# Half of one late store of an attention kernel, issued by GpSimd in seven pieces of 17 rows

## The chip, the cores and the metric

The kernel runs on one core of a Trainium2 chip. The time is that of one execution on the device, in microseconds (us); a median of several runs is given with its range.

## The reference

Cross-covariance attention over 8 batches and 12 heads, 512 positions, 64 channels. The attention matrix of a head is only 64 x 64: the columns of Q and K are normalised over the positions, multiplied, put through a softmax, and the rows of V are multiplied by the result.

```python
Q_norm = Q / (np.linalg.norm(Q, axis=-2, keepdims=True) + 1e-10)
K_norm = K / (np.linalg.norm(K, axis=-2, keepdims=True) + 1e-10)
attn = np.einsum('bhnd,bhne->bhde', Q_norm, K_norm)
attn = np.exp(attn - np.max(attn, axis=-1, keepdims=True))
attn = attn / (np.sum(attn, axis=-1, keepdims=True) + 1e-10)
return np.einsum('bhnd,bhde->bhne', V, attn)
```

All tensors are float32. Q, K and V together are 37.75 MB to read, the output is 12.58 MB to write.

## The kernel before

The 96 heads are taken in 24 units of four heads, two units to a step s (12 steps), two steps to a wide step w of V (6 of them). A step loads Q and K (`qk32`), casts them to bf16 on DVE (`cast_qk`), and multiplies them on PE into Gram matrices (`grams`), which hold both the norms and the products. DVE, ACT and GpSimd turn these into the softmax weights `ab` (`squares` to `normalise`; GpSimd does `scale_k`, the tile `kqs`). V is cast to bf16, mostly by GpSimd (`cast_v`), transposed on PE (`vtrans`) and copied back (`vcopy`). `outs` multiplies it by `ab` into PSUM, and `ocopy` copies the result to the tiles `so` in SBUF, two copies to a tile, on ACT or, late in the program, also on DVE.

A step has two such tiles, i = 0 and 1, and each leaves in one transfer by SP's queue (`store`): 128 partitions, and on each two rows r = 0 and 1 of 2,048 bytes (J = 8 positions of 64 channels), 512 KB in all. Only the last tile, (11, 1), leaves as two transfers of half that size. There are thirteen buffers for `so`, so from store (5, 1) on, the last thirteen, no buffer is used again.

The order in which every engine issues its work is made by a planner, the class `Order`: each piece has costs, predecessors and a due time, and the planner writes out one order for all engines. It reckons with at most eight transfers in flight (`QUEUE = 8`). In the built program, too, each transfer of SP's waits, before it is issued, for the transfer eight before it, whose completion count it takes over. All loads are issued by SP, but two at the start by ACT. GpSimd issues none. At the end of the program SP waits for all the transfers that are still out.

```python
def store(s, i, k=None):
    rows = slice(None) if k is None else slice(k * (J // 2), (k + 1) * (J // 2))
    o = Of[s // 2, s % 2, i].rearrange("p r (j d) -> p r j d", d=D)
    nc.sync.dma_start(out=o[:, :, rows], in_=so[s, i][:, :, rows])
```

Of the kernel before, what the change touches and what calls it, by code (L numbers as in the profile page):

```python
# [102 lines left out]
def kernel(  # L103
# [7 lines left out]
    nc = tc.nc  # L111
# [3 lines left out]
    S = U // 2  # L115
# [3 lines left out]
    ONE = 3  # L119
    HELD, UNTIL = ("lk", 1, 1), ("cq", 0, 1)  # L120
    BOTH = S - 8

# [36 lines left out]
    qk32, v32, vb, qkb, gram, scr, kq, n2, r8, kqs, rq, lg, ex, ab, vps, vt, po, so = ({} for _ in range(18))  # L161
# [35 lines left out]
    def store(s, i, k=None):  # L197
        rows = slice(None) if k is None else slice(k * (J // 2), (k + 1) * (J // 2))
        o = Of[s // 2, s % 2, i].rearrange("p r (j d) -> p r j d", d=D)
        nc.sync.dma_start(out=o[:, :, rows], in_=so[s, i][:, :, rows])  # L200

    def cast_qk(u, x):
# [138 lines left out]
    for i in range(NB["ab"]):  # L341
        a = const.tile([128, HU, 2 * D], BF16, name=f"ab{i}")
# [17 lines left out]
    def piece(key, engines, after, behind, rank, fn, *args):  # L360
        if key[0] in ("cv", "vc", "oc", "kq", "sc"):
            plan.add(key, engines, after, behind, rank, lambda eng: fn(eng, *args))
        else:
            plan.add(key, engines, after, behind, rank, lambda eng: fn(*args))

    def back(kind, i, n, *rest):
        return (kind, i - n, *rest) if i - n >= 0 else None
# [17 lines left out]
    for u in range(U):  # L385
        s, r = divmod(u, 2)
# [21 lines left out]
    for w in range(W):  # L408
        both = 2 * w >= BOTH
        for r in range(2):  # L410
# [24 lines left out]
    for s in range(S):  # L435
        for x in range(4):
            i, k = divmod(x, 2)
            n = 4 * s + x - 2
            wait = [("oc", n // 4, n % 4)] if n >= 0 else []
            order = [("ou", s, x - 1) if x else back("ou", s, 1, 3)]  # L440
            piece(("ou", s, x), {"PE": 0.5}, [("vc", s // 2, *t) for t in turns(s // 2) if t[0] // 2 == k] + [("nm", s)] + wait, order, R["ou"] + 0.01 * s, outs, s, x)
            n = 2 * s + i - NB["so"]
            free = [("st", n // 2, n % 2)] if k == 0 and n >= 0 else []
            order = [("oc", s, x - 1) if x else back("oc", s, 1, 3)]
            piece(("oc", s, x), {"ACT": 0.6, "DVE": (0.68, BIAS["oc"])} if s >= BOTH else {"ACT": 0.6}, [("ou", s, x)] + free, order, R["oc"] + 0.01 * s, ocopy, s, x)
        for i in range(2):
            order = [("st", s, 0) if i else back("st", s, 1, 1)]
            if (s, i) == (S - 1, 1):

                piece(("sh", s, i), {"DMA": 0.67}, [("oc", s, 2)], order, v_at(2 * s + i) + ST_LAG, store, s, i, 0)  # L450
                piece(("st", s, i), {"DMA": 0.67}, [("oc", s, 3)], [("sh", s, i)], v_at(2 * s + i) + ST_LAG, store, s, i, 1)
            else:
                piece(("st", s, i), {"DMA": X}, [("oc", s, 2 * i), ("oc", s, 2 * i + 1)], order, v_at(2 * s + i) + ST_LAG, store, s, i)
# [43 lines left out]
```

## Time and profile before

| | |
|---|---|
| median of 3 runs | 128.83 us (128.76 to 129.06) |
| profiled execution, its own time | 129.06 us |
| its span in the profile | 127.3 us |
| busy: PE, DVE, ACT, POOL (GpSimd) | 62%, 73%, 57%, 28% of the span |
| moved by the DMA engines | 50.64 MB, mean 398 GB/s |
| transfers `out_dram<-so` by SP | 23 of 512 KB, two of 256 KB |
| last copy into `so` ends | 115.4 us |
| last issue of a store by SP | 117.3 us |

The profile shows one execution. Its page has the busy time of each engine, the span in 40 slices of 3.18 us (digits are tenths of a slice, 9 is 90% or more), the DMA queues, and the groups of instructions that cost most. A table of windows gives the same for chosen stretches, in us from the start of the span, with the mean share of time in which the sixteen DMA engines were busy; 1.05 stands for all of them, as the records of consecutive packets overlap a little. The time line lists instructions in order of time. "SPq" is SP issuing transfers; the time up to their landing is not in it.

### The profile page before, as it was taken

To read this page: it belongs to the slowest core of one execution; us is meant where nothing else is said; L and a number is where in the kernel's file an instruction comes from. 1 tells how busy PE (TensorE), PEld (TensorE's weight loads), DVE (VectorE), ACT (ScalarE), POOL (GpSimd) and SP (SyncE) were. 2 spreads that over 40 slices of the span, in tenths; PEclk is the share of its full clock that TensorE was granted. 3 is DMA by queue.
4 is the path that set the end of the run, shared out by engine and by line. 5 is a ranking of instruction groups with operands and counts; after the bars stand their busy time and mean duration, and the time that the engine had idled before them with its cause. 6 is when DMAs were issued, how large, how long until landed. Compare 5 with 4: busy or idle time off the path is not lost.

```text
span 127.3 us, 4884 instructions
## 1 busy us (share of the span) xinstructions
PE 79.4 (62%) x2128; PEld 64.0 (50%) x2128; DVE 93.0 (73%) x141; ACT 72.5 (57%) x220; POOL 36.3 (28%) x40
## 2 busy tenths in 40 slices
PE   0065384894844589859873996698975869580000
PEld 0055372773633568648661885486764748460000
DVE  3263649959999899998986798999999799820000
ACT  4000441569777068785792789384949969972000
POOL 4005306300915913033064203213453361200000
PEclk9999999999997556995999589655699995955555
DMA  3999999999999999999999999999999999999992
GB/s 107 404 434 409 430 409 418 415 440 402 425 429 416 407 418 424 407 416 422 430 415 409 417 424 417 417 420 424 406 413 407 406 401 406 400 407 407 408 352 98
DMA packets 15605, 50.64 MB, mean 398 GB/s; under 512 B 1120, under 2 KB 1632, under 8 KB 14176
## 3 DMA queue, kind: packets, MB, share of 16 engines
q1 hardware_dynamic: 15296, 49.29, 96.2%
q10 hardware_dynamic: 288, 1.05, 2.1%
q8 instruction: 16, 0.26, 0.7%
q14 instruction: 5, 0.04, 0.1%
HBM read 37.75 MB, written 12.58 MB: 396 GB/s over the span
## 4 chain that ended last, share of the span: by engine, by line
DVE 31%; DMA 20%; PE 18%; ACT 14%; issue 4%; SPq 2%; POOL 1%; DVEq 0%; POOLq 0%; ACTq 0%
DMA qk<-in_K_dram 14%; PE gram L226 12%; DVE qkb L206 11%; DVE scr L233 6%; DMA qk<-in_Q_dram 5%; DVE ab L284 5%; ACT so L165 4%; ACT vt L165 4%; ACT ex L275 4%; PE vps L295 3%; DVE vt L167 3%; DVE n L245 3%; PE po L312 2%; ACT kq L165 1%; SPq L184 1%
## 5 line engine op out<-in xcount | busy, mean ns | idle before, releaser
L226 PE MATMUL gram<-qkb 32*128 32x128 bf16 (+1 forms) x1504 | 35.6, 255 | 21.9 <-DVE qkb L206 8.8
L206 DVE CAST qkb<-qk 128x1024 bf16<-128x1024 f32 x48 | 37.3, 801 | 8.5 <-DMA qk<-in_Q_dram 7.0
L226 PEld LDWEIGHTS <-qkb 32*128 32x128 bf16 (+1 forms) x1504 | 29.8, 114 | 26.8 <-DVE qkb L206 11.6
L169 POOL TENSOR_SCALAR vb<-v 128x1024 bf16<-128x1024 f32 x19 | 21.2, 1126 | 45.1 <-DMA v<-in_V_dram 45.0
L165 ACT COPY so<-po 128x512 f32<-128x512 f32 x45 | 25.0, 593 | 6.6 <-PE po L312 6.4
L165 ACT COPY vt<-vps 128x1024 bf16<-128x1024 bf16 (+1 forms) x18 | 17.8, 987 | 15.9 <-PE vps L295 15.9
L312 PE MATMUL po<-ab,vt 128*64 128x128 bf16 x384 | 21.1, 259 | 6.0 <-issue 2.4
L295 PE MATMUL vps<-identb,vb 128*128 128x128 bf16 x192 | 19.3, 255 | 5.1 <-POOL vb L169 3.1
L256 POOL TENSOR_TENSOR kqs<-kq,r 64x512 f32<-64x512 f32 x12 | 13.7, 1143 | 26.9 <-ACT r L252 13.7
L312 PEld LDWEIGHTS <-vt 128*64 128x64 bf16 x384 | 15.3, 131 | 10.3 <-issue 5.4
L233 DVE SCALAR_TENSOR_TENSOR scr<-gram,eye 64x512 f32<-64x512 f32 x24 | 16.5, 688 | 4.7 <-PE gram L226 4.4
L295 PEld LDWEIGHTS <-vb 128*128 128x128 bf16 x192 | 14.1, 113 | 9.0 <-POOL vb L169 4.5
L275 ACT ACTIVATE ex<-lg,rq 128x64 f32<-128x64 f32 x48 | 14.5, 321 | 2.8 <-PE lg L269 2.8
L165 ACT COPY kq<-gram 64x512 f32<-64x512 f32 x12 | 7.0, 580 | 13.6 <-DVE scr L233 13.4
L284 DVE TENSOR_TENSOR ab<-ex,rinv 64x256 bf16<-64x256 f32 x24 | 13.2, 548 | 0.6
L275 ACT ACTIVATION_READ_ACCUMULATOR ex<-lg,rq 128x1 f32 x48 | 10.2, 213 | 0.0
L167 DVE CAST vb<-v 128x1024 bf16<-128x1024 f32 x5 | 7.4, 1483 | 1.3 <-DMA v<-in_V_dram 1.2
L269 PE MATMUL lg<-eye,kqs 64*128 64x64 f32 x48 | 6.9, 274 | 2.3 <-POOL kqs L256 1.8
L245 DVE TENSOR_REDUCE n<-scr 128x8 f32<-128x512 f32 x12 | 8.2, 679 | 0.1
L167 DVE COPY vt<-vps 128x1024 bf16<-128x1024 bf16 (+1 forms) x8 | 7.9, 1019 | 0.1
L269 PEld LDWEIGHTS lg<-eye,kqs 64*128 64x128 f32 x48 | 4.8, 168 | 4.3 <-POOL kqs L256 2.5
L281 DVE RECIPROCAL rinv<-esum 128x4 f32<-128x4 f32 x12 | 2.1, 172 | 2.6 <-ACT ex L275 2.5
(17 smaller groups left out, 16.0 us busy)
## 6 DMA issues: line engine op xcount, KB each, us to landing
out_dram<-so SPq DMA_DIRECT2D x23, 512.0 KB, 10.2
v<-in_V_dram SPq DMA_DIRECT2D x11, 1024.0 KB, 17.2
qk<-in_Q_dram SPq DMA_DIRECT2D x8, 1024.0 KB, 17.5
qk<-in_K_dram SPq DMA_DIRECT2D x8, 1024.0 KB, 18.5
qk<-in_Q_dram SPq DMA_DIRECT2D x8, 512.0 KB, 12.2
qk<-in_K_dram SPq DMA_DIRECT2D x6, 512.0 KB, 12.4
qk<-in_K_dram ACTq DMA_DIRECT2D x2, 512.0 KB, 6.3
v<-in_V_dram SPq DMA_DIRECT2D x2, 512.0 KB, 10.6
```

The source lines that it names most:

```text
L165: nc.scalar.copy(o, i)
L167: nc.vector.tensor_copy(o, i)
L169: nc.gpsimd.tensor_scalar(out=o, in0=i, scalar1=1.0, scalar2=0.0, op0=ALU.mult, op1=ALU.add)
L206: nc.vector.tensor_copy(qkb[u][:, :, x * D:(x + 1) * D], qk32[s][:, x, r])
L226: nc.tensor.matmul(gram[s][:, h, r, 0], x, x, start=(t == 0), stop=(t == (T if u < WIDE else J) - 1))
L233: nc.vector.scalar_tensor_tensor(out=scr[s][half], in0=gram[s][half, :, :, 0, half].rearrange("p h r d -> p (h r) d"), scalar=1e-20, in1=e ...
L245: nc.vector.tensor_reduce(out=n2[s], in_=scr[s], axis=mybir.AxisListType.X, op=ALU.add)
L256: (nc.vector if eng == "DVE" else nc.gpsimd).tensor_tensor(out=kqs[s][HI], in0=kq[s][HI], in1=r8[s][HI, :, None].to_broadcast([D, 2 * HU, ...
L275: nc.scalar.activation(e[:, h, :], lg[s][:, h, :], AF.Exp, scale=rq[s][:, h:h + 1], accum_out=z[:, h:h + 1])
L284: nc.vector.tensor_tensor(out=a[half, :, half], in0=e[half], in1=ri[half, :, None].to_broadcast([D, HU, D]), op=ALU.mult,)
L295: nc.tensor.transpose(ps[:, c, n, :], vb[w][:, J * c + j].rearrange("p r d -> p (r d)"), identb)
L312: nc.tensor.matmul(po[s, x][e * D:(e + 1) * D, j].rearrange("p r d -> p (r d)"), v, ab[s][:, h, :])
```

## The change

The store of tile (9, 1), the sixth transfer from the end, is split. S is 12, so `FEW` is (9, 1). Of its row r = 0, the partitions 0 to 118 go out in seven transfers of 17 partitions, issued by GpSimd; the partitions 119 to 127 go in one transfer by SP. The row r = 1 goes with all 128 partitions in one transfer by SP. The planner still plans one store at this place, and all other stores are as they were.

```diff
     BOTH = S - 8
+    FEW = (S - 3, 1)
...
     def store(s, i, k=None):
         rows = slice(None) if k is None else slice(k * (J // 2), (k + 1) * (J // 2))
         o = Of[s // 2, s % 2, i].rearrange("p r (j d) -> p r j d", d=D)
+        if (s, i) == FEW:
+
+            for a in range(0, 119, 17):
+                nc.gpsimd.dma_start(out=o[a:a + 17, 0], in_=so[s, i][a:a + 17, 0])
+            nc.sync.dma_start(out=o[119:, 0], in_=so[s, i][119:, 0])
+            nc.sync.dma_start(out=o[:, 1], in_=so[s, i][:, 1])
+            return
         nc.sync.dma_start(out=o[:, :, rows], in_=so[s, i][:, :, rows])
```

## The prediction

> **What bounds the kernel now.** I read the page first: the slices, then the table of the DMA queues.
>
> ```profile
> PE   0065384894844589859873996698975869580000
> DVE  3263649959999899998986798999999799820000
> DMA  3999999999999999999999999999999999999992
> q1 hardware_dynamic: 15296, 49.29, 96.2%
> q8 instruction: 16, 0.26, 0.7%
> ```
>
> From the second slice to the last but one, the sixteen DMA engines are full, while every compute engine is idle for the last four slices (12.7 us). The bytes set the time. One engine moves 409/16 = 25.6 GB/s (next view), so a packet of 2,048 bytes costs it 0.08 us, and a store of 512 KB (sixteen such packets on each engine) 1.28 us. Row q8 is instruction fetching: 0.7% of 16 x 127.3 us is 14.3 us in 16 packets, 0.9 us each, on single engines. That is the one thing here that isn't spread evenly.
>
> Second, the end in windows (from:to, then the engines, then the clock, the DMA share and GB/s):
>
> ```profile
> 120.00:122.00 2.00, 0.00 (x0) 0.00 (x0) 0.00 (x0) 0.00 (x0) 0.00 (x0) 0.50 1.05 404
> 122.50:123.00 0.50, 0.00 (x0) 0.00 (x0) 0.00 (x0) 0.00 (x0) 0.00 (x0) 0.50 0.96 358
> 123.00:123.50 0.50, 0.00 (x0) 0.00 (x0) 0.00 (x0) 0.00 (x0) 0.00 (x0) 0.50 0.80 299
> 123.50:124.00 0.50, 0.00 (x0) 0.00 (x0) 0.00 (x0) 0.00 (x0) 0.00 (x0) 0.50 0.68 260
> 124.00:124.50 0.50, 0.00 (x0) 0.00 (x0) 0.00 (x0) 0.00 (x0) 0.00 (x0) 0.50 0.55 205
> 124.50:125.00 0.50, 0.00 (x0) 0.00 (x0) 0.00 (x0) 0.00 (x0) 0.00 (x0) 0.50 0.53 186
> 125.00:125.50 0.50, 0.00 (x0) 0.00 (x0) 0.00 (x0) 0.00 (x0) 0.00 (x0) 0.50 0.55 195
> 125.50:126.00 0.50, 0.00 (x0) 0.00 (x0) 0.00 (x0) 0.00 (x0) 0.00 (x0) 0.50 0.22 74
> ```
>
> A share of 1.05 is all sixteen. At 124 us it is 0.55, so 16 x 0.55/1.05 = 8.4: eight engines are done and eight still work at full rate, until about 125.8 us. The sixteen completion counts of the last store in the trace say the same: eight arrive between 123.10 and 124.60 us, eight between 125.87 and 126.29. Sixteen fetches of 0.9 us, if they fall twice on each of eight engines, give 1.8 of the 2.4 us between the two means (123.7 and 126.1). The kernel ends when the late eight do. The mean of all sixteen is 124.9 us: perfect balance could give 126.3 - 124.9 = 1.4 us and no more.
>
> Third, when the moved work can start, from the time line (start, length):
>
> ```profile
> 107.83 1.04 POOL L256 TENSOR_TENSOR kqs<-kq,r 64x512 f32<-64x512 f32 x1 [3.75 <-ACT r L252]
> 108.65 1.07 ACT L165 COPY so<-po 128x512 f32<-128x512 f32 x2
> ```
>
> The order of the program shows that nothing moves on PE, DVE or ACT. GpSimd gets seven transfers behind its last instruction, which ends at 108.9 us. They wait for the second of the two ACT copies, which fills store (9, 1) and ends at 109.7. So they start at 109.8, beside 12.5 us in which the engines are full anyway. (The line shows the two copies as a group of x2; 108.65 + 1.07 is the end of the second.)
>
> **The change part by part.** The bytes stay the same. Before, every engine had 16 rows of store (9, 1), eight of each half. After, the second half still goes eight to an engine. The first half, 128 rows, goes as 119 in seven transfers of 17, and 9.
>
> No transfer of before has fewer than 128 rows, so no row shows where these go. The bounds: a transfer of 17 rows is spread (one or two rows per engine, and the balance stays), or sits on one engine (17 x 0.08 = 1.36 us of work). The nearest row is the q8 packet, which does sit on one engine. I take the second, and seven different engines for the seven. The nine rows of SP add at most one row to an engine, as one row can't be split further than a packet.
>
> The Trainium skill (DMA: Bandwidth & Descriptors, "Why a DMA increments its semaphore by 16 and not by 1") says that the number of engines is the largest up to 16 that divides the row count: 1 for 17, 9 for 9, and that GpSimd's transfers take consecutive engines in turn while SP's take the lowest-numbered. It also names an exception in which GpSimd gives each engine the row count over 16, rounded up: two rows here, so nine engines. By the first rule seven engines gain 10 rows; by the second eight gain 7. No run here shows either.
>
> So each of seven engines has 17 rows instead of 8 (+9), or +10 with one of SP's nine: +0.72 to +0.80 us. Each of the other nine engines loses 8, or 7 with a row of SP's: -0.64 to -0.56 us.
>
> If the seven are all among the early eight, the early ones end at 124.60 + 0.80 = 125.40 at worst, the late ones at 126.29 - 0.64 to - 0.56, that is 125.65 to 125.73. The late ones still end last, and the gain is 0.6 us.
>
> Issuing on GpSimd: no transfer of GpSimd's is in the trace. Nearest rows: SP's issues of the same tile, 0.37 us at the shortest, and GpSimd's own instructions of 1.04 to 1.14 us. I take 1.0, the engine's own row: 7 x 1.0 from 109.8 ends at 116.8. That costs nothing: the early engines are busy until 122.7 with queued stores, and the extra rows only have to be there before that. Cover is lost at (122.7 - 109.8)/7 = 1.84 us each.
>
> SP: two transfers in place of one. SP issues each transfer only when the one eight before it has landed, which is why its issues in the last stretch stand 1.28 us apart (109.56, 110.84, 112.17). One more transfer takes one of these eight places, so everything behind, stores (10, 0) to (11, 1), is issued one landing later: the last at 118.6 instead of 117.3. An early engine reaches the last store at 122.4, 3.8 us later. In the first slice 107 GB/s x 3.18 us = 340 KB moved, 0.8 us at 420 GB/s, so packets flowed by 2.4 us after an issue at 0.7: 1.7 us. That fits under 3.8, and costs nothing; without it the last store would start late by the difference.
>
> The end: SP closes with one wait after another, 0.06 us apart in the trace. Seven new completion counts, waited for in pairs, add up to four waits, 0 to 0.24 us if they stand behind the last landing. I take 0.12.
>
> Sum: -0.60 + 0.12 = -0.48 us. The profiled execution took 129.06 us (span 127.3 and 1.8 around it), so 128.58; it lay 0.23 over the median of 128.83, so against that 128.35 us.
>
> A rule against the change stands in the same page of the Trainium skill ("Rules for kernel authors"): spreading transfers over issuing engines brings no bandwidth, since they share the sixteen DMA engines. The row of 1.05 agrees that there is no bandwidth to win, and by the rule alone the gain would be zero; but the rows behind 122.5 us show unequal ends, which the rule doesn't speak of.
>
> **The rivals.** First, the seven transfers hit late engines. No view carries an engine's number. For the forecast: early and late are eight and eight, as if one half of the engines did the fetching, and seven loaded engines fit inside the other half, if they are taken in order from its start. Against: if the fetching engines are spread between the others, or are the half that is taken first, at least one late engine is loaded. One suffices: 125.87 to 126.29 + 0.72 to 0.80, at most 0.80 over today's end. With 0.12 for the waits that is 128.83 + 0.92 = 129.75 us, slower. It decides from the first late engine in the set.
>
> Second, the 17 rows are spread over all engines, or so that one of the latest is not relieved: the balance hardly moves, 0 to +0.24 for the waits, 128.8 to 129.0.
>
> Third, GpSimd issues slowly (it hasn't issued one in this program before). Above 1.84 us each it ends the kernel: at 2.5 us the last is out at 109.8 + 17.5 = 127.3, its 1.36 us of rows end at 128.7 where 125.8 was the end, +2.9, 131.7 us. For it speaks nothing but the absence of a row.
>
> **How the numbers follow.** A measurement of this kernel can tell about 0.2% (0.26 us) from no change. Forecast 0.48: the time lies in 128.1 (-0.64, no wait, and the 0.07 by which the fastest run lies under the median) to 128.5. Rival one 0.34, rival two 0.12, rival three 0.06. Rival two gives 0.10 to "same" and 0.02 to "slower"; so faster 0.48, same 0.10, slower 0.42. The range for eight in ten has to reach rival one: 128.1 to 129.85; it leaves out rival three and the edges.
>
> **What would show it.** Right: the DMA share stays at 1.05 to about 123, later than now on the early side, and falls to zero by 125.2 to 125.3 instead of 125.8; a new queue with 119 packets of 2,048 bytes; GpSimd's issues done by 117; SP's last issue near 118.6. Wrong by rival one: a few engines alone busy to 126.6, a share of 0.1 to 0.4 behind 125.8. Wrong by rival two: the same windows as now. Wrong by rival three: GpSimd issuing behind 122 us, and a gap before the last packets.

## The result and the profile after

The changed kernel took 129.16 us (median of 11 runs, 128.97 to 129.28), the kernel before, on the same chip, 128.88 us (128.76 to 129.06): a ratio of 1.0017, interval 1.0009 to 1.0024. By the ratio it is 0.22 us slower (0.12 to 0.31 by its interval; the medians lie 0.28 us apart). The forecast had been 0.48 us faster. The time lies in the range, on the other side of no change.

The profiled execution took 129.17 us, with a span of 127.4. First the table of the DMA queues, with GpSimd's new queue q0, and the group of its issues:

```profile
q1 hardware_dynamic: 15186, 49.04, 95.6%
q8 instruction: 16, 0.26, 0.7%
q0 software_dynamic: 224, 0.24, 0.5%
L204 POOL DMA_DIRECT2D out_dram<-so x7 | 3.7, 541 | 1.1 <-ACT so L166 1.1
```

The 224 packets of q0 are 32 for each of the seven transfers. By size in the trace, each has eight packets of 4,096 bytes, one of 2,052, seven of 8 and sixteen of 4. So a transfer of 17 rows did not leave as 17 rows on one engine: the sizes fit eight engines that took two rows each and a ninth that took one. Issuing took 0.51 us a transfer (0.7 for the first), from 111.7 to 115.4 us, and the rows had landed by 120.0: this part is off the path, as forecast.

Then the end, in windows (from:to, the engines, the clock, the DMA share, GB/s):

```profile
122.50:123.00 0.50, 0.00 (x0) 0.00 (x0) 0.00 (x0) 0.00 (x0) 0.00 (x0) 0.50 1.01 379
123.50:124.00 0.50, 0.00 (x0) 0.00 (x0) 0.00 (x0) 0.00 (x0) 0.00 (x0) 0.50 0.75 277
124.00:124.50 0.50, 0.00 (x0) 0.00 (x0) 0.00 (x0) 0.00 (x0) 0.00 (x0) 0.50 0.70 252
124.50:125.00 0.50, 0.00 (x0) 0.00 (x0) 0.00 (x0) 0.00 (x0) 0.00 (x0) 0.50 0.61 217
125.00:125.50 0.50, 0.00 (x0) 0.00 (x0) 0.00 (x0) 0.00 (x0) 0.00 (x0) 0.50 0.35 121
125.50:126.00 0.50, 0.00 (x0) 0.00 (x0) 0.00 (x0) 0.00 (x0) 0.00 (x0) 0.50 0.15 53
126.00:126.50 0.50, 0.00 (x0) 0.00 (x0) 0.00 (x0) 0.00 (x0) 0.00 (x0) 0.50 0.01 4
```

Up to 125 us the share is higher than before (0.70 against 0.55 at 124): early engines work longer. From 125 to 126 it is lower (0.35 against 0.55, 0.15 against 0.22): most late engines stop sooner. But 0.15 is still 16 x 0.15/1.05 = 2.3 engines, and the last row now reaches past 126. The completion counts of the last store in the trace (one from each engine, when its share has landed) say it by engine: six at 125.38 to 125.67, one at 126.00, and two at 126.41 and 126.43. Before, the eight late ones stood at 125.87 to 126.29. So six late engines were relieved by about 0.6 us, as forecast, and a pair was not. The one at 126.00 got rows too: followed back as the third from the last of each store (125.35, 124.70, 123.43, 122.16, 120.90), it leads to 120.40, the third from the last of the nine counts of SP's transfer of nine rows. The experiments below will show only two late engines among these nine, so it is the slowest of the early ones.

### The profile page after: what moved, and what is told of

It reads as the page before. It is cut to its first block, busy times and chain, and to the rows that moved or that the text cites. A ratio compares the mean times of both kernels' runs of the same rounds, so it can differ in the third digit from the quotient of the medians.

```text
span 127.4 us, 4896 instructions
## 1 busy us (share of the span) xinstructions
PE 78.3 (61%) x2128; PEld 64.4 (51%) x2128; DVE 90.7 (71%) x141; ACT 72.3 (57%) x220; POOL 40.8 (32%) x47
## 3 DMA queue, kind: packets, MB, share of 16 engines
q10 hardware_dynamic: 288, 1.05, 2.2%
## 4 chain that ended last, share of the span: by engine, by line
DVE 37%; PE 31%; issue 12%; ACT 6%; DMA 5%; SPq 0%; DVEq 0%; ACTq 0%
PE gram L234 17%; DVE qkb L214 17%; DVE scr L241 8%; PE po L320 7%; DMA qk<-in_Q_dram 5%; PE vps L303 5%; DVE ab L292 5%; DVE vt L168 3%; DVE n L253 2%; ACT so L166 2%; ACT vt L166 2%; PE lg L277 1%; DVE so L168 1%; ACT ex L283 1%; ACT kq L166 1%
## 5 line engine op out<-in xcount | busy, mean ns | idle before, releaser
L234 PE MATMUL gram<-qkb 32*128 32x128 bf16 (+1 forms) x1504 | 37.0, 262 | 25.5 <-DVE qkb L214 10.5
L234 PEld LDWEIGHTS <-qkb 32*128 32x128 bf16 (+1 forms) x1504 | 31.4, 117 | 29.9 <-DVE qkb L214 12.9
L170 POOL TENSOR_SCALAR vb<-v 128x1024 bf16<-128x1024 f32 x19 | 22.4, 1193 | 32.2 <-DMA v<-in_V_dram 29.0
L303 PE MATMUL vps<-identb,vb 128*128 128x128 bf16 x192 | 18.0, 246 | 3.5 <-POOL vb L170 2.1
L303 PEld LDWEIGHTS <-vb 128*128 128x128 bf16 x192 | 13.5, 110 | 6.6 <-POOL vb L170 2.5
L292 DVE TENSOR_TENSOR ab<-ex,rinv 64x256 bf16<-64x256 f32 x24 | 14.6, 609 | 0.6
L277 PE MATMUL lg<-eye,kqs 64*128 64x64 f32 x48 | 6.4, 258 | 4.2 <-POOL kqs L264 2.2
L204 POOL DMA_DIRECT2D out_dram<-so x7 | 3.7, 541 | 1.1 <-ACT so L166 1.1
```

Of the source, the lines that this page charges most:

```text
L170: nc.gpsimd.tensor_scalar(out=o, in0=i, scalar1=1.0, scalar2=0.0, op0=ALU.mult, op1=ALU.add)
L234: nc.tensor.matmul(gram[s][:, h, r, 0], x, x, start=(t == 0), stop=(t == (T if u < WIDE else J) - 1))
L277: nc.tensor.transpose(l[:, h, :], kqs[s][HI, 2 * h:2 * h + 2].rearrange("p r d -> p (r d)"), eye2[HI])
L292: nc.vector.tensor_tensor(out=a[half, :, half], in0=e[half], in1=ri[half, :, None].to_broadcast([D, HU, D]), op=ALU.mult,)
L303: nc.tensor.transpose(ps[:, c, n, :], vb[w][:, J * c + j].rearrange("p r d -> p (r d)"), identb)
```

## The experiments

Theory A: the kernel ends later because some of the engines that got more rows are among those that end late anyway. Rival B: transfers issued by GpSimd cost time by themselves. Rival C: SP's additional transfer does. All kernels but the last are the changed one with other lines for the first half (r = 0) of store (9, 1); the second half stays with SP unless said otherwise. Every ratio is against runs of the kernel before on the same chip, whose medians were 128.90 to 128.94 us.

**Who issues, with the balance kept.** Two controls, `e_pool128` and `e_sp128`:

```diff
-            for a in range(0, 119, 17):
-                nc.gpsimd.dma_start(out=o[a:a + 17, 0], in_=so[s, i][a:a + 17, 0])
-            nc.sync.dma_start(out=o[119:, 0], in_=so[s, i][119:, 0])
+            nc.gpsimd.dma_start(out=o[0:128, 0], in_=so[s, i][0:128, 0])   # e_pool128
+            nc.sync.dma_start(out=o[0:128, 0], in_=so[s, i][0:128, 0])     # e_sp128
```

> The first half of store (9, 1) leaves by GpSimd in one transfer of 128 rows, eight rows to each DMA engine as before; SP sends the second half. Theory A (the changed kernel is slower because some of the engines that got more rows are among the eight that end late): the balance is that of before, so 128.9 us, within 0.1. Rival B (a transfer issued by GpSimd costs time by itself, whatever its shape): 129.1 us or more, as in the changed kernel.

> SP sends store (9, 1) as two halves of 128 rows; GpSimd sends nothing. Theory A and rival B: 128.9 us, within 0.1, as nothing is uneven and GpSimd is out of it. Rival C (the additional transfer of SP, which takes one of its eight places, costs the time): 129.1 us.

Measured: 129.03 us, ratio 1.0005 (0.9996 to 1.0014), and 128.91 us, ratio 0.9997 (0.9988 to 1.0006). Rival C is out. One transfer by GpSimd costs nothing that can be told.

**Rows on the lowest engines, by SP.** Here SP sends the first half in transfers whose row counts put 17 rows on each of the first seven, six or five engines: `e_sp119` with 119 and 9 rows, `e_sp102` with 102, 16 and 10, `e_sp85` with 85, 32 and 11. The edit for the last:

```diff
-            for a in range(0, 119, 17):
-                nc.gpsimd.dma_start(out=o[a:a + 17, 0], in_=so[s, i][a:a + 17, 0])
-            nc.sync.dma_start(out=o[119:, 0], in_=so[s, i][119:, 0])
+            nc.sync.dma_start(out=o[0:85, 0], in_=so[s, i][0:85, 0])
+            nc.sync.dma_start(out=o[85:117, 0], in_=so[s, i][85:117, 0])
+            nc.sync.dma_start(out=o[117:128, 0], in_=so[s, i][117:128, 0])
```

> The 119 rows leave by SP in one transfer and the nine rows in another; GpSimd sends nothing. In the changed kernel the transfer of nine rows completed in nine counts on nine engines, three of them late. By the Trainium skill (DMA: Bandwidth & Descriptors, Why a DMA increments its semaphore by 16 and not by 1) 119 rows go to the seven lowest-numbered engines, 17 rows each. Theory A: if a late engine is among the engines that take the 119 rows, it gets 17 + 1 rows instead of 8, 10 x 0.08 = +0.8 us: 129.7 us, and the completion counts of this transfer fall into early and late ones. If none is late, 128.3 to 128.5 us. Rival B: 128.9 us, as GpSimd sends nothing.

> The first half leaves by SP as 102, 16 and 10 rows; GpSimd sends nothing. By the Trainium skill (DMA: Bandwidth & Descriptors, Why a DMA increments its semaphore by 16 and not by 1) 102 rows go to the six lowest-numbered engines, 17 each. Theory A: if those six are all early, the other ten engines lose 6 or 7 rows of 0.08 us, 0.5 us, and the six gain 11, 0.9 us, which takes the last early one from 124.6 to 125.5 us in the profile, before the late ones: 128.4 us. If one of the six is late, +0.9 us: 129.8 us. Rival B: 128.9 us.

> The first half leaves by SP as 85, 32 and 11 rows; GpSimd sends nothing. By the Trainium skill (DMA: Bandwidth & Descriptors, Why a DMA increments its semaphore by 16 and not by 1) 85 rows go to the five lowest-numbered engines, 17 each. Theory A: 102 rows on six engines left exactly one engine late, and 119 on seven left two. If the one late engine of the six is the sixth, this kernel loads five early ones (+12 rows of 0.08 us at most, 124.6 to 125.6 us) and takes 5 or 6 rows off the late ones (0.4 to 0.5 us, less what two small transfers cost): 128.5 to 128.8 us. If the late one is among the five, +0.5 us or more: 129.4 us, and one of the five completion counts is late.

Measured: 129.25 us, ratio 1.0026 (1.0016 to 1.0037); 129.50 us, 1.0043 (1.0029 to 1.0056); 128.56 us, 0.9976 (0.9967 to 0.9985). None of the three uses GpSimd, so rival B can't make the first two slower. The transfers of 119, 102 and 85 rows have seven, six and five completion counts in the trace (us):

```
119 rows: 118.10 118.41 118.84 119.35 120.19 | 120.58 120.61
102 rows: 118.28 118.62 119.21 119.56 119.99 | 120.95
 85 rows: 118.21 118.56 118.98 119.47 119.65 |
```

Each is an engine's place in its queue, plus 17 rows (1.37 us). Taken off, the numbers left of the bar are early engines' counts of the store just ahead, those right of it late ones'. (In `e_sp119` the store just ahead has early counts up to 118.85 and late ones from 119.22.) By the Trainium skill (DMA: Bandwidth & Descriptors, "Why a DMA increments its semaphore by 16 and not by 1"), transfers of SP's take the engines from the lowest number: then the first five are early, the sixth and the seventh late. The fifth (118.82 in `e_sp119` when 1.37 is taken off) is the slowest early engine. The counts agree with the section in number (seven, six and five); the engines' numbers themselves are in no row. The windows of the end show the same. First the kernel with 102 rows:

```profile
125.50:126.00 0.50, 0.00 (x0) 0.00 (x0) 0.00 (x0) 0.00 (x0) 0.00 (x0) 0.50 0.08 27
126.00:126.50 0.50, 0.00 (x0) 0.00 (x0) 0.00 (x0) 0.00 (x0) 0.00 (x0) 0.50 0.06 23
126.50:127.00 0.50, 0.00 (x0) 0.00 (x0) 0.00 (x0) 0.00 (x0) 0.00 (x0) 0.50 0.02 6
```

16 x 0.06/1.05 = 0.9: one engine works alone for half a microsecond and more. With 85 rows:

```profile
124.50:125.00 0.50, 0.00 (x0) 0.00 (x0) 0.00 (x0) 0.00 (x0) 0.00 (x0) 0.50 0.72 252
125.00:125.50 0.50, 0.00 (x0) 0.00 (x0) 0.00 (x0) 0.00 (x0) 0.00 (x0) 0.50 0.24 84
125.50:126.00 0.50, 0.00 (x0) 0.00 (x0) 0.00 (x0) 0.00 (x0) 0.00 (x0) 0.50 0.00 0
```

The end is steep, with nobody left behind 125.5. This is the forecast's own idea on the right engines, and it beats both kernels.

Two kernels load fewer engines, `e_sp51` (51, 64 and 13 rows) and `e_sp34` (34, 80 and 14), by the same edit:

> The first half leaves by SP as 51, 64 and 13 rows. By the Trainium skill (same section) 51 rows go to the three lowest-numbered engines, 17 each. A look at which engines are late: if the late one is among these three, one of the first transfer's three completion counts comes over 0.5 us behind the other two, and the last landing is that engine's, 129.4 us; if not, all three are early and the time is 128.6 to 129.0 us.

> The first half leaves by SP as 34, 80 and 14 rows. By the Trainium skill (same section) 34 rows go to the two lowest-numbered engines, 17 each. As with 51 rows: one late count of two and 129.3 us, if one of the two engines is late; else 128.7 to 129.0 us.

One run each: 128.65 and 128.92 us. All three counts of the one (117.94, 118.28, 119.12) and both of the other (118.21, 119.38) are early ones, so no late engine is among the first three. A single run doesn't rank these times.

**The price of GpSimd's transfers.** `e_pool16`:

```diff
-            for a in range(0, 119, 17):
-                nc.gpsimd.dma_start(out=o[a:a + 17, 0], in_=so[s, i][a:a + 17, 0])
-            nc.sync.dma_start(out=o[119:, 0], in_=so[s, i][119:, 0])
+            for a in range(0, 128, 16):
+                nc.gpsimd.dma_start(out=o[a:a + 16, 0], in_=so[s, i][a:a + 16, 0])
```

> GpSimd sends the first half in eight transfers of 16 rows, one row to each engine and transfer, so the balance is that of before. In the runs so far a transfer of SP's with one row per engine took 0.18 to 0.21 us of an engine's time where a packet of 2,048 bytes takes 0.08. Theory A without a price for a transfer: 128.9 us. Theory A with that price for each small transfer of GpSimd's: 8 x 0.1 = +0.8 us, 129.7 us. Rival B (GpSimd's transfers cost by their number): the same 129.7 us, so this run only tells what a small transfer costs.

Measured: 129.07 us, ratio 1.0015 (1.0007 to 1.0024), +0.19 us for eight transfers, 0.024 each (0.01 to 0.04 by the interval). The 0.8 us didn't come. They rested on a misread: the 0.18 to 0.21 us between the counts of two small transfers of SP's are the delay of a count and not an engine's time. In `e_sp85` an engine's count for one row came 0.18 us after the one before, and that for the next eight rows only 0.55 after it: nine rows in 0.73 us, 0.08 each. Rival B is right about a small part, then. Where the 0.19 us sit is open: the two profiled executions, of this kernel and of the kernel before, took the same 129.06 us, with last landings at 126.25 and 126.29, and can't show a difference of the medians.

**GpSimd on the right engines, and twice the change.** `e_pool5` and `e_twice`:

```diff
+            for a in range(0, 85, 5):                                      # e_pool5
+                nc.gpsimd.dma_start(out=o[a:a + 5, 0], in_=so[s, i][a:a + 5, 0])
+            nc.sync.dma_start(out=o[85:117, 0], in_=so[s, i][85:117, 0])
+            nc.sync.dma_start(out=o[117:, 0], in_=so[s, i][117:, 0])
...
+            for r in range(2):                                             # e_twice, both halves
+                for a in range(0, 119, 17):
+                    nc.gpsimd.dma_start(out=o[a:a + 17, r], in_=so[s, i][a:a + 17, r])
+            nc.sync.dma_start(out=o[119:], in_=so[s, i][119:])
```

> GpSimd sends 85 rows of the first half in 17 transfers of five rows, SP the other 43 as 32 and 11. If GpSimd puts one row of each on the five lowest-numbered engines, the rows lie as in the run with 85 rows by SP, which took 0.34 us off. Theory A with GpSimd's price of 0.024 us for a transfer: -0.34 + 17 x 0.024 = +0.07, 128.8 to 129.0 us. Rival B (number of transfers alone): +0.4, 129.3 us. If the transfers hit other engines: 129.3 us or more.

> Both halves of store (9, 1) leave as the first one does in the changed kernel: 14 transfers of 17 rows by GpSimd, and the nine last partitions of both halves by SP. Theory A (two late engines are among the eight that take two rows of every transfer): these two gain 14 rows of 0.08 us, 1.1 us, less the 0.3 to 0.5 us by which they are ahead of the latest, and GpSimd's transfers add 14 x 0.024 = 0.3 us by the run with eight of 16 rows: 129.8 to 130.0 us. Rival B (the number of GpSimd's transfers alone, 0.19 us for eight): 129.2 to 129.3 us.

Measured: 128.73 us, ratio 0.9988 (0.9978 to 0.9997), a little better than expected; and 129.77 us, ratio 1.0070 (1.0054 to 1.0087). With seventeen transfers by GpSimd the kernel is faster than before, with fourteen it is 0.9 us slower. So it is the place of the rows that decides, and not the number of GpSimd's transfers. That GpSimd put its fives on the same five engines is in no row; the last store's counts fit it: three come early, up to 123.38 us, and the others from 124.31 on, as with 85 rows by SP (123.00 and 124.34). The end of `e_twice`:

```profile
125.50:126.00 0.50, 0.00 (x0) 0.00 (x0) 0.00 (x0) 0.00 (x0) 0.00 (x0) 0.50 0.14 47
126.00:126.50 0.50, 0.00 (x0) 0.00 (x0) 0.00 (x0) 0.00 (x0) 0.00 (x0) 0.50 0.13 47
126.50:127.00 0.50, 0.00 (x0) 0.00 (x0) 0.00 (x0) 0.00 (x0) 0.00 (x0) 0.50 0.01 4
```

0.13 is two engines, alone for the last microsecond; their counts come at 126.86 and 126.97, the third last at 125.96. From `e_pool5`, against the run with 85 rows by SP, a transfer of GpSimd's costs about (0.31 - 0.15)/17 = 0.01 us. The intervals of these two ratios overlap, and this price and the 0.024 from the run with eight are not told apart.

**How far it goes.** `e_sp115` has 115 rows (23 on each of the five) and 13, both by SP:

```diff
+            nc.sync.dma_start(out=o[0:115, 0], in_=so[s, i][0:115, 0])
+            nc.sync.dma_start(out=o[115:128, 0], in_=so[s, i][115:128, 0])
```

> SP sends the first half as 115 and 13 rows; by the Trainium skill (DMA: Bandwidth & Descriptors, Why a DMA increments its semaphore by 16 and not by 1) 115 rows are 23 for each of the five lowest-numbered engines. Theory A: the late engines lose 7 or 8 rows, 0.6 us, but the slowest of the five early ones, at 124.6 to 125.3 us without the change, gains 16 rows, 1.3 us, and now ends last, at 125.9 to 126.6: 128.6 to 129.2 us, no better than with 85 rows. If there were room left on the early engines: 128.3 us.

Measured: 128.70 us (128.42 to 129.12), ratio 0.9987 (0.9972 to 1.0001): not told apart from before, nor surely from 85 rows. In the profiled execution, the slowest of the ten with 129.12 us, a single count of the last store comes late, at 126.46, and the fifteen others by 125.68. It leads back store by store to 120.66, the fifth count of the 115 rows. So the slowest early engine has become the bound, in the range expected for it.

**Why eight engines are late.** `e_gram5` is the kernel before with five terms of each Gram sum. It leaves out the others, and with them 1,024 of PE's 2,128 matmuls and their weight loads, so its output is not the reference's:

```diff
-        for t in range(T if u < WIDE else J):
+        for t in range(5):
...
-                nc.tensor.matmul(gram[s][:, h, r, 0], x, x, start=(t == 0), stop=(t == (T if u < WIDE else J) - 1))
+                nc.tensor.matmul(gram[s][:, h, r, 0], x, x, start=(t == 0), stop=(t == 4))
```

> The kernel before, with 5 of every 16 (and of the last unit's 8) terms of the Gram sums kept and the other matmuls left out, so that PE has 2,126 instructions in place of 4,174 and eight packets of 16 KB fewer are fetched. Theory F (the eight late engines are late because each was held up by two instruction fetches): with one fetch for each the gap between early and late halves, 1.2 us: 127.6 to 127.9 us. Rival G (they are late for another reason, such as their place): only the eight fetches' own work goes, 8 x 0.9 / 16 = 0.45 us, and the gap of 2.4 us between early and late stays: 128.4 to 128.9 us.

Measured: 127.66 us, ratio 0.9905 (0.9890 to 0.9919), 1.2 us less. The row of the instruction queue, and the end in windows:

```profile
q8 instruction: 8, 0.13, 0.4%
```

```profile
123.00:123.50 0.50, 0.00 (x0) 0.00 (x0) 0.00 (x0) 0.00 (x0) 0.00 (x0) 0.50 0.79 279
123.50:124.00 0.50, 0.00 (x0) 0.00 (x0) 0.00 (x0) 0.00 (x0) 0.00 (x0) 0.50 0.65 227
124.00:124.50 0.50, 0.00 (x0) 0.00 (x0) 0.00 (x0) 0.00 (x0) 0.00 (x0) 0.50 0.36 127
124.50:125.00 0.50, 0.00 (x0) 0.00 (x0) 0.00 (x0) 0.00 (x0) 0.00 (x0) 0.50 0.03 8
```

With eight fetches in place of sixteen, the plateau of eight engines from 124 to 125.5 us is gone. Between the means of the early and the late eight counts of the last store lie 1.1 us instead of 2.4: the early mean stayed (123.69 and 123.59 us), the late one came down from 126.06 to 124.72. So the fetching of PE's instructions makes the late engines late, about 1.2 us for each fetch (theory F), a little more than the 0.9 us of the packet.

The trace of the kernel before shows the same step by step, in the sixteen counts of each of its loads and stores, taken from the first count of the same transfer. In the loads just ahead of the first fetch (13.66 us) all sixteen lie within 0.6 us. Behind it one lies 1.9 us back, behind the second (21.40) two. Behind the eighth (60.10) eight lie 1.4 to 1.8 back and the others within 0.9. Behind the ninth (66.27) one lies 3.3 back, seven 1.4 to 1.8. Behind the sixteenth (108.68) eight lie 2.8 to 3.2 back and none between 1.7 and 2.7. So the second eight fetches fell on the eight engines that had been held up once.

## Why the prediction was right or wrong

**What bounds the kernel: right.** Sixteen full engines, an end set by the late eight, and the fetches as their cause, which had been only a sum that fitted; `e_gram5` and the steps in the counts of the kernel before showed it. (The 409 GB/s behind the price of a row are those of the windows from 116 to 120 us; the row shown there has 404, which gives the same 0.08 us.)

**Where a transfer of 17 rows goes: wrong.** I took one engine for each transfer, by the nearness to the row of the fetch packet, and so +9 or +10 rows on seven engines. It was two rows on each of eight engines and one on a ninth. This is the exception in the Trainium skill (DMA: Bandwidth & Descriptors, "Why a DMA increments its semaphore by 16 and not by 1") that the prediction cited beside the rule, and the packet sizes of q0 agree with it. With a row of SP's, eight engines have 15 rows instead of 8: +7, 0.56 us. The last counts agree as well: the two earliest of the late eight, at 125.87 and 125.88 us before, would end at 126.43 and 126.44; 126.41 and 126.43 were measured.

**That the loaded engines are all early: the step that failed.** I put half the chance on it, with no row that carried a number. The counts of `e_sp119`, `e_sp102` and `e_sp85` show five early and two late among the first seven. With these two loaded, the relief of the others (0.6 us, as worked out) is worth nothing to the end, which moved from 126.29 to 126.43 us between the two profiles. A smaller miss stands beside it: the loaded early engines were put at 125.40 us at worst, and the slowest of them ended at 126.00. By these counts, even without the two late ones the gain would have been 0.3 us and not 0.6. That the time lies in the stated range is owed to rival one, which the range had to reach, and not to the forecast.

**Rival one: right in its mechanism, wrong in its size**, +0.92 us where 0.22 were measured. It took +10 rows for +7, which is 0.24 us. It put them on top of the latest late engine, but the two loaded ones are ahead of it: in `e_sp119` their counts of the store ahead are 119.22 and 119.23 and the latest is 119.83, 0.6 us; in `e_sp102` the one is 0.3 us ahead (and its 11 more rows, 0.88 us, less 0.3, are 0.58, where 0.55 was measured). And it added 0.12 us for closing waits, which weren't there: from the last landing to the end of the span it is 0.97 us before and 0.96 after, since SP passed all seven of GpSimd's counts before the last landing, six of them in one wait with the count of an earlier store. In their place stands GpSimd's own price, which is known only roughly: 0.01 to 0.024 us a transfer, 0.07 to 0.17 for seven. The sum: 0.56 less a lead of 0.3 to 0.6, and 0.07 to 0.17, is 0.0 to 0.4 us; 0.22 lies in it. `e_twice` checks the first term: another 7 rows made it 0.9 - 0.22 = 0.7 us worse, where 0.56 and seven more transfers give 0.63 to 0.73.

**Work named as hidden: right.** GpSimd's issues took 0.51 us where 1.0 was taken, and ended long before the early engines ran dry. They began at 111.7 us and not at 109.8:

```profile
109.59 1.04 POOL L264 TENSOR_TENSOR kqs<-kq,r 64x512 f32<-64x512 f32 x1 [4.33 <-ACT r L260]
111.69 3.71 POOL L204 DMA_DIRECT2D out_dram<-so  x7 [1.06 <-ACT so L166]
```

In this execution GpSimd's last instruction came 1.8 us later than in the profile before, and the issues then waited for ACT's copy; neither mattered. SP's last issue moved from 117.3 to 118.95 us (118.6 forecast). `e_sp128`, with its last issue at 118.5, shows that such a shift costs nothing, and `e_sp85`, at 120.2, is still faster than before.

**Rivals two and three** fall: the windows did change, and GpSimd wasn't slow.

## What to carry to other kernels

When the DMA engines are full and their ends are unequal, the shares of the last windows give both the most there is to gain (the mean against the latest) and how many engines are late. Which ones must be measured before rows are moved: a transfer that runs on few engines, put behind a large store, tells it by its completion counts. One late engine among those that get more is enough to turn the gain round, so the best set may be smaller than the early set: five engines here, for -0.24% (0.9976, 0.9967 to 0.9985).

## What was not expected of the hardware

The sixteen fetches of PE's instructions held up eight of the sixteen DMA engines, twice each, and in `e_gram5`, with eight fetches, the gap was half. If SP's transfers take the engines from the lowest number, these eight are no block: two are the sixth and seventh, the eighth and ninth are early (their first counts for the nine rows in `e_sp119` are 116.77 and 116.81 us), so six of the other seven are late. And GpSimd and SP place few rows differently: 17 rows by GpSimd were on nine engines, while 85 and 119 rows by SP were on five and seven, with 17 rows each.
